# One staging pool for both MLP products, three staging buffers, and another order in the MLP's first block

## The chip, the cores and the metric

The kernel runs on one core of a Trainium2 chip. The metric is the device time of one execution in microseconds. Before the change the median of three runs is 2079.51 us (2078.61 to 2080.41). One further execution was profiled; its rows are what the prediction reads.

The engines that matter are TensorE (PE, with its weight loads shown as PEld), VectorE (DVE), ScalarE (ACT) and SyncE (SP). SP only issues transfers, in the order of its queue: an issue that has to wait for a semaphore holds all that stand behind it.

## The reference, cut to what matters

One layer on 512 tokens with a model width of 2048 and a hidden width of 8192, all float32. Only the convolution mixer is used.

```
h = rms_norm(x, norm_mix)
b, c, v = split(h @ conv_w_in, 3)          # 2048 -> 3 x 2048
m = (b * conv3(c * v)) @ conv_w_out        # 2048 -> 2048
x = x + m
h = rms_norm(x, norm_mlp)
x = x + square(relu(h @ mlp_w1)) @ mlp_w2  # 2048 -> 8192 -> 2048
```

## The kernel before, in words

**Numbers in two halves.** A float32 product is made of three matmuls. Each operand is split into a rounded half "hi" (ACT, line 101) and the remainder "lo" (DVE, line 102), and hi x hi, lo x hi and hi x lo are added up in PSUM. Activations appear in the profile as h, g and f (fhi, flo), weights as r, split into whi and wlo. The split weights live in a ring of three pairs (RING).

**The mixer.** The input projection (lines 284 to 317) and the output projection (lines 330 to 350) use plain products in pieces of 256 output columns. The output projection has eight such blocks. Each adds the residual, scales by the norm's gain, splits the slices of three activation forms, writes the other four forms to DRAM (t_mid, line 348) and adds the squares of the new x to ssq (line 113).

**The MLP's products.** Both MLP products use a Strassen-Winograd scheme of seven quarter products (function `fast`) for a 2 x 2 split of weights and activations. The weights' forms are X11, S1, S2, S4, S3, X12, X22, the activations' forms Y11, T1, T2, Y22, T3, Y21, T4, matched in this order. A quarter product has 8 steps of three matmuls, so 24; a block of 256 output columns has 168. The sums of the weights are made on the fly on DVE (`quarters`, line 173). The first product has 32 blocks (line 368), the second 32 as well: four chunks of the hidden width with eight blocks each.

**Forms of the activations.** Seven forms, each a pair hi and lo of 128 x 2048, have one home each (fa and fb). For the first product Y11, Y21, Y22 are split slice by slice in the output projection, while T1 to T4 are read back from t_mid. For the second product all seven forms of a chunk are read from `hidden`, which the first product's blocks write (line 378): chunk 0 from blocks 0 to 7, and so on. A read (function `read`, line 356) goes into a staging tile f of 1 MB and is split from there into its home. A home can be written once the last matmul with its old contents is done.

**Norm.** The second norm's factor per token (rbc) is not applied to h but to the first product's result (line 372). `token_factors` makes it: one matmul with a matrix of ones adds ssq over the partitions (line 119, the "squares' matmul"), then mean, square root and reciprocal follow with one step of refinement on DVE.

**Buffers.** The first product's block has a result c (two buffers), which is rescaled (line 372), squared into q (line 374), extended by differences (line 217) and written to hidden. Before the change the tiles f and q of the first product share one tag "q" with two buffers in the pool mw. The second product has a pool of its own, vw, opened after mw is closed and lying over the same memory: two buffers for f, two for the residual xt, two for c, and one for the output staging o.

**What sets the order.** The framework plans each engine's order by program order and by when, in its own timing, an instruction's inputs and its buffer are there. So the weight splits of a later block can stand ahead of an earlier block's last steps. On the chip each engine then goes through its list in order, held only by semaphores.

Of the kernel before, what the change touches and what calls it, by code (L numbers as in the profile page):

```python
# [36 lines left out]
def trunk_kernel(  # L37
# [47 lines left out]
    edge.tile([P, 120], F32, name="edge")  # L85
    ident = cst.tile([P, P], F32, name="ident")
    ones = cst.tile([P, P], F32, name="ones")
    rows = cst.tile([5 * KT, P], F32, name="rows")
# [26 lines left out]
    def token_factors(pool):  # L115


        total = bank()
        pe.matmul(total, ones, ssq, start=True, stop=True)
        m = pool.tile([P, S], F32, tag="sq", name="m")  # L120
        t = pool.tile([P, S], F32, tag="sq", name="t")
        dve.tensor_scalar(m, total, 1.0 / D, RMS_EPS, op0=ALU.mult, op1=ALU.add)
        act.activation(t, m, AF.Sqrt)
        dve.reciprocal(rbc, t)
# [3 lines left out]
        dve.tensor_tensor(out=rbc, in0=rbc, in1=t, op=ALU.mult)  # L128
# [58 lines left out]
    def fast(r, forms, c):  # L187
# [5 lines left out]
        for i, (hi, lo) in quarters(r):  # L193
# [31 lines left out]
    cw = es_h.enter_context(tc.tile_pool(name="cw", bufs=2))  # L225

# [19 lines left out]
    with tc.tile_pool(name="xin", bufs=2, side="right", reuse_waits="tile") as xin:  # L246
# [30 lines left out]
        token_factors(cw)  # L277
# [78 lines left out]
    def read(i, src, pool):  # L356

        f = pool.tile([P, NP, HS], F32, tag="q", name="f")
# [5 lines left out]
    with tc.tile_pool(name="mw", bufs=2, reuse_waits="tile") as mw:  # L364
        for i, k in ((T1, 0), (T2, 1), (T3, 2), (T4, 3)):
            forms[i] = read(i, t_mid[:, :, k, :], mw)
        token_factors(mw)
        for n in range(DFF // GC):
            c = mw.tile([P, 2, S], F32, tag="c", name="c")
            fast(load(w1, 0, n * GC), forms, c)  # L370
            r = rbc.unsqueeze(1).to_broadcast([P, 2, S])
            dve.scalar_tensor_tensor(out=c, in0=c, scalar=0.0, in1=r, op0=ALU.max, op1=ALU.mult)
            q = mw.tile([P, 8, HS], F32, tag="q", name="q")
            act.activation(
                q[:, :4, :].rearrange("p q t -> p (q t)"), c.rearrange("p i t -> p (i t)"), AF.Square
            )
            differences(q)
            nc.sync.dma_start(hidden[n // NP][n % NP], q)

    with tc.tile_pool(name="vw", bufs=2, reuse_waits="tile") as vw:  # L380
        def finish(n, c):

            o = vw.tile([P, S // P, GC], F32, tag="o", name="o", bufs=1)
            for b in range(0, S // P, 2):
                pt = bank()
                for i in range(2):
                    for j in range(2):
                        pe.transpose(  # L388
                            pt[:, i * GC + j * P : i * GC + (j + 1) * P],
                            c[:, j, (b + i) * P : (b + i + 1) * P], ident,  # L390
                        )
                act.copy(o[:, b : b + 2, :].rearrange("p b c -> p (b c)"), pt)
            act.dma_start(out[:, n * GC : (n + 1) * GC].rearrange("(b p) c -> p b c", p=P), o)

        done = None
        for ch in range(NCH):
            for i in range(7):
                forms[i] = read(i, hidden[ch][:, :, PLACE[i], :], vw)
            for n in range(NG):
                xt = vw.tile([P, 2, S], F32, tag="xt", name="xt")  # L400
                nc.sync.dma_start(xt.rearrange("p i t -> p (i t)"), x_mid[ch][n])
                c = vw.tile([P, 2, S], F32, tag="c", name="c")
                fast(load(w2, ch * D, n * GC), forms, c)
                dve.tensor_tensor(out=c, in0=c, in1=xt, op=ALU.add)
                if ch < NCH - 1:
                    nc.sync.dma_start(x_mid[ch + 1][n], c.rearrange("p i t -> p (i t)"))
                else:
                    if done:
                        finish(*done)
                    done = n, c  # L410
        finish(*done)


# [28 lines left out]
```

## Time and profile before

| What | us |
|---|---|
| median of three runs | 2079.51 |
| profiled execution | 2078.44 |
| its span, from the first to the last instruction | 2076.7 |
| PE busy | 2025.4 |
| DVE busy | 1418.0 |
| ACT busy | 840.1 |

A row of the timeline has start, length, engine, line, operation, output and inputs, count, and in brackets the idle time before it with what ended it. A row of the waits has the waiting instruction, what it waited for, the total in us, how many times and the longest. A row of the windows has the length of a stretch, and for each engine the busy time and in parentheses the number of instructions; then PE's granted clock as a share of full speed, the DMA engines' busy share and the rate. A row of the groups has the total and after it the mean in ns of one instruction, then the idle time before it.

### The profile page before, as it was taken

The numbers are of one execution on the slowest core, as the hardware profiler recorded it, in microseconds if no ns is written. First come the engines' busy times: TensorE is split into PE (matmuls) and PEld (weight loads), VectorE is DVE, ScalarE is ACT, GpSimd is POOL, SyncE is SP. The second block draws the span as 40 slices with busy tenths as digits, with TensorE's granted clock in tenths as the row PEclk, the third lists the DMA queues.
The fourth block names the chain that finished last, engine by engine and source line by source line (L and its number), as shares of the span: only waits on it lengthen the run. The fifth ranks groups of instructions, "written<-read, shape, count | busy, mean of one in ns | idle before, by whom it ended". The sixth has DMA issues, their size and how long they took to land.

```text
span 2076.7 us, 32835 instructions
## 1 busy us (share of the span) xinstructions
PE 2025.4 (98%) x14001; PEld 1896.6 (91%) x14001; DVE 1418.0 (68%) x1541; ACT 840.1 (40%) x1036; POOL 0.7 (0%) x6
## 2 busy tenths in 40 slices
PE   9999999999999889999999999969999999999998
PEld 7888888888888789999999999968999999999998
DVE  6643333433444588888888887868779779779875
ACT  5322222222333354444444444435445446446443
POOL 0000000000000000000000000000000000000000
PEclk9999999999999999999999999989999999999999
DMA  8323223232354444453434444366448448447441
GB/s 284 122 81 116 87 84 120 81 107 96 131 184 149 163 165 160 148 179 144 163 143 162 164 148 177 143 207 232 148 166 279 168 159 288 163 143 255 141 153 62
DMA packets 260114, 325.13 MB, mean 157 GB/s; under 512 B 9008, under 2 KB 242560, under 8 KB 255872
## 3 DMA queue, kind: packets, MB, share of 16 engines
q1 hardware_dynamic: 255616, 318.80, 44.7%
q10 hardware_dynamic: 4352, 4.24, 0.6%
q8 instruction: 109, 1.79, 0.3%
q14 instruction: 37, 0.30, 0.0%
HBM read 260.09 MB, written 62.91 MB: 156 GB/s over the span
## 4 chain that ended last, share of the span: by engine, by line
PE 92%; DVE 3%; DMA 3%; ACT 1%; issue 1%; SPq 0%; DVEq 0%; ACTq 0%
PE acc L199 20%; PE acc L200 20%; PE acc L198 20%; PE acc L154 11%; PE acc L155 11%; PE acc L153 11%; DMA f<-hidden 1%; DVE flo L102 1%; DVE wlo L102 1%; DMA r<-in_conv_w_in_dram 1%; ACT fhi L101 0%; DVE s L173 0%; DMA r<-in_mlp_w_dram 0%; PE acc L388 0%; ACT whi L101 0%
## 5 line engine op out<-in xcount | busy, mean ns | idle before, releaser
L198 PE MATMUL acc<-fhi,whi 128*128 128x256 f32 x3584 | 1019.2, 285 | 22.4 <-ACT fhi L101 21.1
L199 PE MATMUL acc<-flo,whi 128*128 128x256 f32 x3584 | 1018.0, 284 | 9.5 <-DVE flo L102 9.5
L200 PE MATMUL acc<-fhi,wlo 128*128 128x256 f32 x3584 | 1017.4, 284 | 4.1 <-DVE wlo L102 4.1
L102 DVE TENSOR_TENSOR wlo<-r,whi 128x1024 fp32r<-128x1024 f32 x384 | 468.9, 1223 | 399.2 <-ACT whi L101 389.6
L198 PEld LDWEIGHTS acc<-fhi,whi 128*128 128x128 f32 x3584 | 691.4, 193 | 24.9 <-ACT fhi L101 21.9
L101 ACT CAST whi<-r 128x1024 fp32r<-128x1024 f32 x384 | 403.4, 1051 | 758.2 <-PE acc L154 372.0
L199 PEld LDWEIGHTS acc<-flo,whi 128*128 128x128 f32 x3584 | 691.8, 193 | 11.1 <-DVE flo L102 10.6
L200 PEld LDWEIGHTS acc<-fhi,wlo 128*128 128x128 f32 x3584 | 691.4, 193 | 5.3 <-DVE wlo L102 5.3
L101 ACT CAST whi<-s 128x1024 fp32r<-128x1024 f32 x192 | 201.4, 1049 | 323.0 <-PE acc L199 222.1
L154 PE MATMUL acc<-h_lo,whi 128*128 128x512 f32 x768 | 298.9, 390 | 0.9 <-DVE h_lo L268 0.6
L155 PE MATMUL acc<-h_hi,wlo 128*128 128x512 f32 x768 | 298.8, 389 | 0.3 <-DVE wlo L102 0.3
L153 PE MATMUL acc<-h_hi,whi 128*128 128x512 f32 x768 | 297.8, 390 | 0.6 <-ACT h_hi L267 0.5
L102 DVE TENSOR_TENSOR wlo<-s,whi 128x1024 fp32r<-128x1024 f32 x192 | 234.2, 1222 | 60.9 <-ACT whi L101 60.9
L154 PEld LDWEIGHTS acc<-h_lo,whi 128*128 128x128 f32 x768 | 144.1, 188 | 32.3 <-DVE h_lo L268 2.2
L153 PEld LDWEIGHTS acc<-h_hi,whi 128*128 128x128 f32 x768 | 143.8, 188 | 31.3 <-ACT h_hi L267 1.3
L155 PEld LDWEIGHTS acc<-h_hi,wlo 128*128 128x128 f32 x768 | 144.1, 188 | 30.3 <-DVE wlo L102 0.5
L211 DVE TENSOR_TENSOR c<-acc,c 128x256 f32<-128x256 f32 x192 | 81.4, 424 | 100.3 <-PE acc L200 96.8
L153 PE MATMUL acc<-g_hi,whi 128*128 128x512 f32 x256 | 99.6, 389 | 0.0
L154 PE MATMUL acc<-g_lo,whi 128*128 128x512 f32 x256 | 99.6, 389 | 0.0
L155 PE MATMUL acc<-g_hi,wlo 128*128 128x512 f32 x256 | 99.6, 389 | 0.0
L102 DVE TENSOR_TENSOR flo<-f,fhi 128x2048 fp32r<-128x2048 f32 x32 | 73.2, 2287 | 15.0 <-ACT fhi L101 14.9
L173 DVE TENSOR_TENSOR s<-r 128x1024 f32<-128x1024 f32 x64 | 78.0, 1219 | 4.2 <-DMA r<-in_mlp_w_dram 2.8
(66 smaller groups left out, 1005.1 us busy)
## 6 DMA issues: line engine op xcount, KB each, us to landing
r<-in_mlp_w_dram SPq DMA_DIRECT2D x256, 512.0 KB, 5.5
r<-in_conv_w_in_dram SPq DMA_DIRECT2D x96, 512.0 KB, 5.7
hidden<-q SPq DMA_DIRECT2D x32, 1024.0 KB, 3.8
f<-hidden SPq DMA_DIRECT2D x28, 1024.0 KB, 6.2
r<-in_conv_w_out_dram SPq DMA_DIRECT2D x32, 512.0 KB, 5.3
xt<-x_mid SPq DMA_DIRECT2D x32, 512.0 KB, 4.1
x_mid<-c SPq DMA_DIRECT2D x24, 512.0 KB, 2.9
xn<-in_x_dram SPq DMA_DIRECT2D x16, 256.0 KB, 5.1
```

The costliest lines, as they stand in the source:

```text
L101: act.copy(hi, src)
L102: dve.tensor_tensor(out=lo, in0=src, in1=hi.bitcast(F32), op=ALU.subtract)
L153: pe.matmul(acc[j], hi[:, k, cs], a, start=first, stop=False)
L154: pe.matmul(acc[j], hi[:, k, cs], b, start=False, stop=False)
L155: pe.matmul(acc[j], lo[:, k, cs], a, start=False, stop=last)
L173: dve.tensor_tensor(out=o, in0=a, in1=b, op=op)
L198: pe.matmul(acc, hi[:, k, :], f_hi[:, k, :], start=first, stop=False, skip_group_check=True)
L199: pe.matmul(acc, hi[:, k, :], f_lo[:, k, :], start=False, stop=False, skip_group_check=True)
L200: pe.matmul(acc, lo[:, k, :], f_hi[:, k, :], start=False, stop=last, skip_group_check=True)
L211: dve.tensor_tensor(out=o, in0=acc, in1=o, op=ALU.add)
```

## The change

- The pool mw stays open to the end and serves both products. Its tag "q" now has three buffers and holds f, q and the output staging o. c and xt are tags of the same pool. vw is gone.
- `token_factors` is called after the products of the MLP's first block instead of before them, and takes the tag "xt" for its two temporaries.
- In the MLP's first block only (`early`), X12 with Y21 comes second instead of sixth.
- To make room, `rows` moves into the pool cw, which is closed before the MLP, and a padding tile ("edge") shrinks from 120 to 8 columns.

```diff
-    edge.tile([P, 120], F32, name="edge")
+    edge.tile([P, 8], F32, name="edge")
-    rows = cst.tile([5 * KT, P], F32, name="rows")
...
-    def token_factors(pool):
+    def token_factors(pool, tag):
         total = bank()
         pe.matmul(total, ones, ssq, start=True, stop=True)
-        m = pool.tile([P, S], F32, tag="sq", name="m")
-        t = pool.tile([P, S], F32, tag="sq", name="t")
+        m, t = (pool.tile([P, S], F32, tag=tag, name=n) for n in ("m", "t"))
...
-    def quarters(r):
+    def quarters(r, early):
...
         yield X11, operand(x11, shape)
+        if early:
+            yield X12, operand(x12, shape)
         tt(s_b, s_a, x11)
...
-        yield X12, operand(x12, shape)
+        if not early:
+            yield X12, operand(x12, shape)
         yield X22, operand(x22, shape)
...
     cw = es_h.enter_context(tc.tile_pool(name="cw", bufs=2))
+    rows = cw.tile([5 * KT, P], F32, name="rows", bufs=1)
...
-        f = pool.tile([P, NP, HS], F32, tag="q", name="f")
+        f = pool.tile([P, NP, HS], F32, tag="q", name="f", bufs=3)
...
-    with tc.tile_pool(name="mw", bufs=2, reuse_waits="tile") as mw:
-        for i, k in ((T1, 0), (T2, 1), (T3, 2), (T4, 3)):
-            forms[i] = read(i, t_mid[:, :, k, :], mw)
-        token_factors(mw)
-        for n in range(DFF // GC):
+    mw = ctx.enter_context(tc.tile_pool(name="mw", bufs=2, reuse_waits="tile"))
+    for i, k in ((T1, 0), (T2, 1), (T3, 2), (T4, 3)):
+        forms[i] = read(i, t_mid[:, :, k, :], mw)
+    for n in range(DFF // GC):
+        c = mw.tile([P, 2, S], F32, tag="c", name="c")
+        fast(load(w1, 0, n * GC), forms, c, early=n == 0)
+        if n == 0:
+            token_factors(mw, "xt")
...
+        q = mw.tile([P, 8, HS], F32, tag="q", name="q", bufs=3)
...
-    with tc.tile_pool(name="vw", bufs=2, reuse_waits="tile") as vw:
...
-            o = vw.tile([P, S // P, GC], F32, tag="o", name="o", bufs=1)
+        o = mw.tile([P, S // P, GC], F32, tag="q", name="o", bufs=3)
...
-                forms[i] = read(i, hidden[ch][:, :, PLACE[i], :], vw)
+            forms[i] = read(i, hidden[ch][:, :, PLACE[i], :], mw)
-                xt = vw.tile([P, 2, S], F32, tag="xt", name="xt")
+            xt = mw.tile([P, 2, S], F32, tag="xt", name="xt")
-                c = vw.tile([P, 2, S], F32, tag="c", name="c")
+            c = mw.tile([P, 2, S], F32, tag="c", name="c")
```

More of the change, by code (lines that the diff above doesn't have):

```diff
@@ L183, in quarters, with fast @@
         yield S3, operand(x21, shape)
-        yield X12, operand(x12, shape)
+        if not early:
+            yield X12, operand(x12, shape)
         yield X22, operand(x22, shape)
-    def fast(r, forms, c):
+    def fast(r, forms, c, early=False):
         bx, by, bz = (bank()[:, :HS] for _ in range(3))
@@ L192, in fast @@
         t0, t1 = slice(0, HS), slice(HS, S)
-        for i, (hi, lo) in quarters(r):
+        for i, (hi, lo) in quarters(r, early):
             acc = sums[i]
@@ L276, in trunk_kernel @@
                 unit(acc_n[i], r_n[i], c * XK, h_hi, h_lo, k_first=c == 0)
-        token_factors(cw)
+        token_factors(cw, "sq")
     with tc.tile_pool(name="gp", bufs=1, side="right", reuse_waits="tile") as gp:
@@ L362, in read @@
         return made
-    with tc.tile_pool(name="mw", bufs=2, reuse_waits="tile") as mw:
-        for i, k in ((T1, 0), (T2, 1), (T3, 2), (T4, 3)):
-            forms[i] = read(i, t_mid[:, :, k, :], mw)
-        token_factors(mw)
-        for n in range(DFF // GC):
-            c = mw.tile([P, 2, S], F32, tag="c", name="c")
[L370 to L378, printed above, removed]
@@ L380, in trunk_kernel @@
-    with tc.tile_pool(name="vw", bufs=2, reuse_waits="tile") as vw:
-        def finish(n, c):
-            o = vw.tile([P, S // P, GC], F32, tag="o", name="o", bufs=1)
[L384 to L397, printed above, removed]
-                forms[i] = read(i, hidden[ch][:, :, PLACE[i], :], vw)
-            for n in range(NG):
-                xt = vw.tile([P, 2, S], F32, tag="xt", name="xt")
-                nc.sync.dma_start(xt.rearrange("p i t -> p (i t)"), x_mid[ch][n])
-                c = vw.tile([P, 2, S], F32, tag="c", name="c")
[L403 to L411, printed above, removed]
@@ new lines, in trunk_kernel @@
+    mw = ctx.enter_context(tc.tile_pool(name="mw", bufs=2, reuse_waits="tile"))
[6 more added lines that the diff above has]
+            token_factors(mw, "xt")
+        r = rbc.unsqueeze(1).to_broadcast([P, 2, S])
+        dve.scalar_tensor_tensor(out=c, in0=c, scalar=0.0, in1=r, op0=ALU.max, op1=ALU.mult)
+        q = mw.tile([P, 8, HS], F32, tag="q", name="q", bufs=3)
+        act.activation(
+            q[:, :4, :].rearrange("p q t -> p (q t)"), c.rearrange("p i t -> p (i t)"), AF.Square
+        )
+        differences(q)
+        nc.sync.dma_start(hidden[n // NP][n % NP], q)
@@ new lines, in finish @@
+    def finish(n, c):
+        o = mw.tile([P, S // P, GC], F32, tag="q", name="o", bufs=3)
+        for b in range(0, S // P, 2):
+            pt = bank()
+            for i in range(2):
+                for j in range(2):
+                    pe.transpose(
+                        pt[:, i * GC + j * P : i * GC + (j + 1) * P],
+                        c[:, j, (b + i) * P : (b + i + 1) * P], ident,
+                    )
+            act.copy(o[:, b : b + 2, :].rearrange("p b c -> p (b c)"), pt)
+        act.dma_start(out[:, n * GC : (n + 1) * GC].rearrange("(b p) c -> p b c", p=P), o)
@@ new lines, in trunk_kernel @@
+    done = None
+    for ch in range(NCH):
+        for i in range(7):
+            forms[i] = read(i, hidden[ch][:, :, PLACE[i], :], mw)
+        for n in range(NG):
+            xt = mw.tile([P, 2, S], F32, tag="xt", name="xt")
+            nc.sync.dma_start(xt.rearrange("p i t -> p (i t)"), x_mid[ch][n])
+            c = mw.tile([P, 2, S], F32, tag="c", name="c")
+            fast(load(w2, ch * D, n * GC), forms, c)
+            dve.tensor_tensor(out=c, in0=c, in1=xt, op=ALU.add)
+            if ch < NCH - 1:
+                nc.sync.dma_start(x_mid[ch + 1][n], c.rearrange("p i t -> p (i t)"))
+            else:
+                if done:
+                    finish(*done)
+                done = n, c
@@ L415 @@
+    finish(*done)
 _INS = [
```

## The prediction

> **What bounds the kernel now.** I read the busy times first, then the waits of the matmul engine, then windows over the places where it waits.
>
> ```profile
> PE 2025.4 (98%) x14001; PEld 1896.6 (91%) x14001; DVE 1418.0 (68%) x1541; ACT 840.1 (40%) x1036; POOL 0.7 (0%) x6
> ...
> PE acc L198 <- ACT fhi L101: 21.1, 4, 16.9
> PE acc L119 <- DVE ssq L113: 5.0, 1, 5.0
> ```
>
> PE is the bound nearly everywhere, so only its holes can be won. The largest are waits for a split operand (fhi); one is the squares' matmul waiting for its sum. Windows size each hole (columns: start and end, length, then busy time and count of PE, PEld, DVE, ACT, POOL, granted clock, DMA share, GB/s):
>
> ```profile
> 770.00:1370.00 600.00, 600.00 (x5002) 600.00 (x5002) 497.84 (x568) 279.51 (x359) 0.00 (x0) 1.00 0.44 157
> ...
> 715.60:752.30 36.70, 25.60 (x171) 24.12 (x171) 32.00 (x33) 18.06 (x20) 0.00 (x0) 0.86 0.46 158
> 1357.10:1427.20 70.10, 46.54 (x338) 45.24 (x337) 47.60 (x45) 31.53 (x31) 0.00 (x0) 0.81 0.64 215
> 1548.30:1611.90 63.60, 61.28 (x504) 60.47 (x504) 59.98 (x53) 37.74 (x40) 0.00 (x0) 1.00 0.80 264
> 1709.80:1773.50 63.70, 62.55 (x517) 61.90 (x516) 60.53 (x53) 38.88 (x41) 0.00 (x0) 1.00 0.82 272
> 1871.00:1938.00 67.00, 64.15 (x525) 62.98 (x524) 61.54 (x54) 38.31 (x41) 0.00 (x0) 1.00 0.67 222
> ```
>
> Undisturbed, a matmul takes 600/5002 = 0.12 us, a block of 168 takes 20.16, a quarter product of 24 takes 2.88. Length minus count times 0.12 is what each stretch loses: entry of the MLP (first MLP block) 16.2 us, first product to second 29.5, and the three later changes of hidden chunk 3.1, 1.7 and 4.0. Each of these five places is touched by the change.
>
> **Part 1: the first MLP block.** The kernel before puts the squares' matmul (L119) ahead of X11.
>
> ```profile
> 716.78 0.41 DVE L102 TENSOR_TENSOR flo<-q,fhi 128x256 fp32r<-128x256 f32 x1
> 718.58 0.75 DVE L102 TENSOR_TENSOR flo<-q,fhi 128x256 fp32r<-128x256 f32 x2
> 720.66 1.81 PE L119 MATMUL acc<-ssq,ones 128*128 128x512 f32 x2 [4.95 <-DVE ssq L113]
> 729.91 0.39 PE L198 MATMUL acc<-fhi,whi 128*128 128x256 f32 x1 [3.67 <-ACT fhi L101]
> 732.76 0.58 PE L199 MATMUL acc<-flo,whi 128*128 128x256 f32 x1 [2.47 <-DVE flo L102]
> ...
> 720.03 0.34 SPq L348 DMA_DIRECT2D t_mid<-q  x1
> 722.79 13.11 SPq L359 DMA_DIRECT2D f<-t_mid  x4
> ...
> 727.95 1.90 ACT L101 CAST fhi<-f 128x2048 fp32r<-128x2048 f32 x1 [0.48 <-DMA f<-t_mid]
> 730.62 1.90 ACT L101 CAST fhi<-f 128x2048 fp32r<-128x2048 f32 x1 [0.77 <-DMA f<-t_mid]
> ...
> 724.35 3.35 DVE L124 RECIPROCAL rbc<-t 128x512 f32<-128x512 f32 x1 [0.74 <-ACT t L123]
> 730.42 2.29 DVE L102 TENSOR_TENSOR flo<-f,fhi 128x2048 fp32r<-128x2048 f32 x1
> ...
> L128 DVE TENSOR_TENSOR rbc<-rbc,t 128x512 f32<-128x512 f32 x2 | 1.4, 692 | 0.1
> L102 DVE TENSOR_TENSOR wlo<-r,whi 128x1024 fp32r<-128x1024 f32 x384 | 468.9, 1223 | 399.2 <-ACT whi L101 389.6 <-PE acc L264 6.6 <-PE acc L119 2.4
> ```
>
> The output projection ends at 720.66 - 4.95 = 715.7. X11 needs Y11, whose last slice is there at 717.2, and X11 reaches that slice only after 21 matmuls, at 718.2. So X11 and X12 (Y21's last slice at 719.3) run 715.7 to 721.5. The chain that ends the hole does not move: last differences written at 720.03, T1 requested at 722.79, cast to 729.85, low part from 730.42 (0.5 us sooner if VectorE is free) to 732.7. PE then stands 721.5 to 732.5, and S1 starts as before. X12's 24 matmuls no longer stand behind S1: -2.9, and up to -0.5 from the low part. The squares' matmul costs PE nothing if it falls into the gap between S1's first and second matmul, where its bank is next; 0.9 (half of 1.81) if it comes last.
>
> X12's operands move ahead of S1's in the ring of three: X11, X12, S1 are split while the projection still runs, S2 and S4 take the places of X11 and X12 at 718.6 and 721.5, inside the hole. If that cover were gone, a split of 1.05 + 1.22 would show.
>
> The norm's chain on VectorE is the reciprocal (3.35) and five operations of at most 0.69: up to 6.8. It began while PE stood. Now it needs the squares' matmul, which comes after S1's first, so it runs inside the block, and the weight splits and the rescale of the first c are queued behind it. From 730 to 752 VectorE has four low parts (9.2), the chain (6.8), five weight splits (6.1) and about 2.5 of sums and additions (estimated as two more such splits): 24.6 in 22. So 0 to 2.6 come back; I take 1. If the whole chain were exposed, 6.8 would. Part 1: **-2.4**, between -3.9 and +3.9. T3 no longer waits for a buffer, but PE has no hole at T3 now, so that is worth nothing; the work that hides it is S1 and S2.
>
> **Part 2: first product to second.** Now f of hidden chunk 0 lies in a pool that opens over the first product's buffers.
>
> ```profile
> 1365.44 0.34 SPq L378 DMA_DIRECT2D hidden<-q  x1
> 1371.05 2.63 SPq L136 DMA_DIRECT2D r<-in_mlp_w_dram  x4
> 1384.54 0.34 SPq L378 DMA_DIRECT2D hidden<-q  x1
> 1384.98 5.04 SPq L359 DMA_DIRECT2D f<-hidden  x2
> ...
> 1396.66 20.84 SPq L359 DMA_DIRECT2D f<-hidden  x5
> ...
> 1380.82 1.06 ACT L374 ACTIVATE q<-c 128x1024 f32<-128x1024 f32 x1 [2.16 <-DVE c L372]
> ...
> 1384.06 0.42 DVE L217 TENSOR_TENSOR q<-q 128x256 f32<-128x256 f32 x1
> ...
> 1396.69 0.58 PE L199 MATMUL acc<-flo,whi 128*128 128x256 f32 x1 [1.75 <-DVE flo L102]
> 1406.99 0.57 PE L199 MATMUL acc<-flo,whi 128*128 128x256 f32 x1 [2.26 <-DVE flo L102]
> ...
> 1407.00:1410.40 3.40, 3.40 (x16) 3.40 (x17) 3.28 (x2) 0.31 (x1) 0.00 (x0) 0.51 0.61 189
> ...
> hidden<-q SPq DMA_DIRECT2D x32, 1024.0 KB, 3.8
> f<-hidden SPq DMA_DIRECT2D x28, 1024.0 KB, 6.2
> ```
>
> The first read of chunk 0, whose data were written 23 blocks earlier, stands on SP behind the last write of hidden (1384.54), and the other five each wait for one of two buffers. With one pool, the order in which the planner hands out buffers of a tag decides. L119 above is the clue: it stands ahead of X11 although X11's operands were complete 3.5 us sooner, so banks are given in order of first use. By that order the first two reads follow the last block's Square (ACT 1380.82) in the plan and go ahead of the last write on SP. SP itself has nothing to wait for there: the previous writes are long landed (1365.44 + 3.8), so they issue when the weight loads are through, at 1373.7.
>
> Two reads of T1 and T2 landed 2.7 us apart (727.95, 730.62), so I estimate 2.7 us per MB. Two MB of weights from 1371.05 and two of f land at about 1380 and 1383. ACT does Square until 1381.9, then the casts until 1383.8 and 1385.7; VectorE is free at 1384.5, the low parts are done at 1386.8 and 1389.1. X11 runs from 1386.8 instead of 1396.69: 9.9 us.
>
> After that, three buffers. X11 at half clock (16 matmuls in 3.4 us by the window row instead of 1.9) ends at 1391.2, S1 at 1394.1. The third read takes the first buffer at 1386.8, lands 6.2 later, and is split 4.2 later, at 1397.2: a hole of 3.1, another 1.5 of half clock, S2 ends at 1401.5. The fourth and fifth were issued at 1388.4 (1384.54 + 3.8) and 1389.1 and are there in time. The sixth and seventh take buffers at 1397.2 and 1399.9 and are ready at 1407.6 and 1410.3; X22 ends at 1413.4. VectorE's work of the stretch (47.60 in 70.10) is squeezed into 58, so I add 2: 1415.4 against 1427.3. Part 2: **-12**, between -6 (reads stay behind the write, third buffer alone) and -26 (the change costs only what a later change of chunk costs).
>
> The Trainium skill, "TensorE: Matmul & The Clock Gate", section "Why this matters for your kernels", lets the clock fall only for gaps over about 3 us. Here a gap of 2.26 us was followed by 3.4 us at clock 0.51, so the measurement decides against it. By the rule the hole of 3.1 us before S2 stands at the edge, and the sum would be up to 1.5 lower.
>
> **Part 3: the three later changes of chunk.**
>
> ```profile
> 1560.00:1600.00 40.00, 37.68 (x308) 36.87 (x307) 38.45 (x34) 24.45 (x25) 0.00 (x0) 1.00 0.98 326
> ...
> ACT fhi L101 <- DMA f<-hidden: 4.4, 2, 2.8
> ...
> ACT fhi L101 <- DMA f<-hidden: 7.1, 4, 2.4
> ```
>
> The reads are already early here. A third buffer removes the casts' waits for them (4.4 and 7.1 us at the first and third change), but VectorE is busy 38.45 of 40 us and DMA 0.98, so little of it reaches PE. Of 8.8 us lost in all I take **-2**, between -6 and +3 (one more read in flight in front of the weights, 1 us each).
>
> **Part 4: the end.** The output staging o has one buffer before and three now.
>
> ```profile
> 2068.82 0.38 ACTq L393 DMA_DIRECT2D out_dram<-o  x1
> 2068.97 1.09 PE L388 MATMUL acc<-ident,c 128*128 128x128 f32 x8 [0.85 <-DVE c L404]
> 2071.68 1.07 ACT L392 COPY o<-acc 128x512 f32<-128x512 f32 x2 [2.88 <-DMA out_dram<-o]
> ```
>
> The last copies wait for the previous output to leave. Without it they start when the first four transposes are through, near 2069.7: **-1.9**, between -2.2 and -1. The moves of rows and of the padding tiles change no instruction: zero, since they are addresses only.
>
> **Sum.** -2.4 - 12 - 2 - 1.9 = -18.3. The profiled execution took 2078.44 (span 2076.7 and 1.7 around it), so it becomes 2060.1; the median of the runs lies 1.07 above the profiled one, so the forecast is 2061.2.
>
> **Rivals.**
> - *Reads far ahead.* If a read takes any free buffer, chunk 0 is staged long before and this change costs 3 us like the others: -26 in part 2, 2047. Against it: three reads taken at block 8 would hold all three buffers until the last block frees the forms, and block 8's q would never get one.
> - *It doesn't do what it says:* the first read is still planned behind the last write (for it: it stands there today, 0.44 us behind). Then only the third buffer counts: -6 in part 2, 2067. Against it: today two pools force that order.
> - *No gain in either MLP place,* the norm's chain exposed (+3.9), part 2 at -6, the later changes at +3, the end -1.9: -1.0, 2078.5. VectorE's load speaks for it; that each price is the far end of its bound speaks against it.
> - *Slower: weight loads stuck behind reads on SP.* A read that waits for its buffer holds the in-order queue (the five reads of the fence hold it 20.84 us). The weights of block 33 are issued at 1371.05; block 33 could start two blocks after 1357.1, at 1397.4, and they need 6 to land and 5 for sums and splits, so about 16 us of lateness is free. It decides from there: held 26 us at each of the last three changes, PE waits 10 each, +30 - 18.3, 2091. Against it: the queue has stood that long already, and a third buffer shortens each wait.
>
> **How the numbers follow.** Forecast 0.70 (own range 2052 to 2069); reads far ahead 0.08; first read still behind 0.12; no gain 0.05; slower 0.05. A measurement of this kernel tells about 0.2% (4 us) from no change, so faster is below 2075.3: 0.70 + 0.08 + 0.12 = 0.90; same 0.05; slower 0.05. The range of 8 in 10 leaves out the far-ahead case and the two bad ones: 2050 to 2070.
>
> **What would show it.** Part 1: X11 directly behind the projection without a wait, L119 in or after S1, one wait of about 11 us before S1, block 1 near 750. Part 2: two reads of hidden on SP ahead of the last write, X11's wait about 9 us instead of 17, then holes under 3 us. Part 3: VectorE still near full at the changes. Part 4: the last copies not waiting for the output. The prediction is wrong if the first read is issued long before block 31, or if reads stand ahead of weights and PE waits for whi.

## The result, and the profile after

| | before | after |
|---|---|---|
| median (lowest to highest), us | 2079.06 (2076.66 to 2080.41) | 2043.93 (2039.87 to 2045.94) |
| profiled execution, us | 2078.44 | 2044.67 |
| its span, us | 2076.7 | 2042.9 |

With one further run, the median before the change is of four. The ratio is 0.983, with a 95% interval of 0.9812 to 0.9848: 35 us faster, where 18 were forecast (2061.2, range 2050 to 2070). The direction was right, the time lies outside the range. The line numbers after the change: the three matmuls of a quarter product are L200 to L202 (L198 to L200 before), the split is L100 and L101 (L101 and L102 before).

Windows show where the 35 us come from. In the kernel before, the first row is a stretch in which PE has no hole, the second the output projection, then the two blocks in which each hidden chunk changes (columns as in the prediction: length, busy time and count of PE, PEld, DVE, ACT, POOL, granted clock, DMA share, GB/s):

```profile
775.00:1330.00 555.00, 555.00 (x4628) 555.00 (x4627) 460.75 (x526) 258.76 (x332) 0.00 (x0) 1.00 0.44 156
541.50:715.50 174.00, 174.00 (x769) 143.93 (x767) 80.28 (x116) 59.02 (x85) 0.00 (x0) 1.00 0.47 163
1568.41:1612.08 43.67, 41.35 (x339) 40.54 (x337) 40.44 (x37) 22.35 (x26) 0.00 (x0) 1.00 0.84 280
1733.04:1775.36 42.32, 41.16 (x338) 40.52 (x337) 40.34 (x37) 22.54 (x26) 0.00 (x0) 1.00 0.87 288
1896.32:1941.76 45.44, 42.59 (x347) 41.42 (x345) 41.28 (x37) 23.10 (x27) 0.00 (x0) 1.00 0.66 216
```

The same view of the kernel after; the third row is its first MLP block, the fourth the two blocks around the change from the first product to the second:

```profile
775.00:1330.00 555.00, 555.00 (x4780) 555.00 (x4778) 473.11 (x543) 267.99 (x343) 0.00 (x0) 1.00 0.45 161
541.60:720.50 178.90, 178.90 (x768) 143.41 (x767) 79.95 (x116) 59.20 (x85) 0.00 (x0) 1.00 0.46 159
720.79:755.75 34.96, 24.81 (x171) 22.41 (x170) 31.52 (x33) 18.01 (x19) 0.00 (x0) 0.85 0.56 195
1341.31:1400.08 58.77, 44.76 (x339) 43.47 (x337) 48.39 (x45) 31.48 (x31) 0.00 (x0) 0.88 0.73 251
1536.77:1584.13 47.36, 42.17 (x339) 41.57 (x338) 41.55 (x38) 21.20 (x25) 0.00 (x0) 0.93 0.75 260
1701.24:1748.62 47.38, 41.77 (x338) 41.17 (x337) 41.51 (x38) 21.51 (x25) 0.00 (x0) 0.93 0.75 259
1865.74:1913.70 47.96, 42.45 (x346) 41.64 (x345) 42.32 (x38) 21.98 (x26) 0.00 (x0) 0.96 0.54 187
```

The first rows hold the surprise. PE is busy without a hole in both, at a granted clock of 1.00, and yet the kernel after does 4780 matmuls in the 555 us and the kernel before 4628: 116.1 ns each instead of 119.9. The matmul itself became faster in the MLP. In the output projection it became slower, 178.90/768 = 232.9 ns against 174.00/769 = 226.3.

The timeline of PE in the kernel after shows that it isn't every matmul (start, length, engine, line). Each row is the first of a step's three; the first two rows belong to X12, with Y21, and stand one step apart, the last two to X22, with T4:

```profile
1357.01 0.28 PE L200 MATMUL acc<-fhi,whi 128*128 128x256 f32 x1
...
1357.37 0.28 PE L200 MATMUL acc<-fhi,whi 128*128 128x256 f32 x1
...
1358.79 0.28 PE L200 MATMUL acc<-fhi,whi 128*128 128x256 f32 x1
...
1359.13 0.28 PE L200 MATMUL acc<-fhi,whi 128*128 128x256 f32 x1
```

Three matmuls with Y21 take 0.36 us, as all did before; three with T4 take 0.34. All three quarters that read Y forms (X11, S4, X12) keep 120 ns, the four that read T forms (S1, S2, S3, X22) run at 113.3. A block is 3 x 24 x 0.1197 + 4 x 24 x 0.1133 = 19.5 us instead of 20.16. T forms and g lie on the right side of the memory, Y forms, h and the split weights on the left. The change moved the sides against each other, as the sizes in the diff tell: `rows`, 128 columns of 4 bytes, left the left side, so all behind it moves by -512 bytes; `edge` lost 112 columns of 4, so all on the right moves by +448. In the kernel before all of them lie a multiple of 512 bytes from the split weights, in a partition. The change takes this offset of T forms and g from 0 to -64 bytes modulo 512. That of Y forms and h stays 0.

With 168 matmuls a block, the length of a window less its blocks at the undisturbed pace (20.16 or 19.52 each) is what a place loses. That gives the account between the two profiled executions:

| place | before, lost | after, lost | difference |
|---|---|---|---|
| 64 blocks at the undisturbed pace | 64 x 20.16 | 64 x 19.52 | -41.0 |
| output projection | 768 x 0.2263 | 768 x 0.2329 | +5.1 |
| first MLP block | 16.6 | 15.4 | -1.1 |
| first product to second | 29.9 | 19.7 | -10.1 |
| three later changes of chunk | 3.4 + 2.0 + 5.1 | 8.3 + 8.3 + 8.9 | +15.1 |
| end, after the last matmul of a block | 9.7 | 7.7 | -2.0 |

The sum is -34.0, the profiled executions differ by 33.8. (Each difference is taken before rounding.)

The change from the first product to the second is nearly as forecast. SP's queue and the timeline of PE of the kernel after:

```profile
1354.92 2.21 SPq L134 DMA_DIRECT2D r<-in_mlp_w_dram  x4
1357.18 4.31 SPq L362 DMA_DIRECT2D f<-hidden  x2
1368.47 0.33 SPq L382 DMA_DIRECT2D hidden<-q  x1
```

```profile
720.54 0.39 PE L153 MATMUL acc<-g_hi,wlo 128*128 128x512 f32 x1
720.77 0.28 PE L200 MATMUL acc<-fhi,whi 128*128 128x256 f32 x1
...
734.56 0.58 PE L200 MATMUL acc<-fhi,whi 128*128 128x256 f32 x1 [7.88 <-ACT fhi L100]
734.94 1.91 PE L118 MATMUL acc<-ssq,ones 128*128 128x512 f32 x2
...
1369.28 0.58 PE L200 MATMUL acc<-fhi,whi 128*128 128x256 f32 x1 [8.29 <-ACT fhi L100]
...
1541.96 0.58 PE L202 MATMUL acc<-fhi,wlo 128*128 128x256 f32 x1 [4.56 <-DVE wlo L101]
```

Two reads stand ahead of the last write, right behind the weight loads. X11 stands directly behind the projection, and the squares' matmul falls behind S1's first. At the end the last copies wait 0.87 us for PE and no longer for the output to leave:

```profile
2037.92 1.07 ACT L395 COPY o<-acc 128x512 f32<-128x512 f32 x2 [0.87 <-PE acc L391]
```

The last row of PE's timeline above is the new loss at a later change of chunk: PE waits 4.56 us for the low part of a weight. VectorE in the kernel after, there:

```profile
1535.15 4.48 DVE L101 TENSOR_TENSOR flo<-f,fhi 128x2048 fp32r<-128x2048 f32 x2
1539.56 1.22 DVE L407 TENSOR_TENSOR c<-c,xt 128x1024 f32<-128x1024 f32 x1
1540.69 1.22 DVE L101 TENSOR_TENSOR wlo<-r,whi 128x1024 fp32r<-128x1024 f32 x1
```

In the kernel before, at the same change, one low part of f stands there, and PE's longest hole is 1.17 us:

```profile
1568.50 2.29 DVE L102 TENSOR_TENSOR flo<-f,fhi 128x2048 fp32r<-128x2048 f32 x1
1570.71 1.22 DVE L404 TENSOR_TENSOR c<-c,xt 128x1024 f32<-128x1024 f32 x1
1571.85 2.35 DVE L102 TENSOR_TENSOR wlo<-s,whi 128x1024 fp32r<-128x1024 f32 x2
```

```profile
1580.06 0.38 PE L200 MATMUL acc<-fhi,wlo 128*128 128x256 f32 x1 [1.17 <-DVE wlo L102]
```

### The profile page after: what moved, and what is told of

Same layout as the page of the kernel before. It is cut to its first block, busy times and chain, and to the rows that moved or that the text cites. A ratio compares the mean times of both kernels' runs of the same rounds, so it can differ in the third digit from the quotient of the medians.

```text
span 2042.9 us, 32807 instructions
## 1 busy us (share of the span) xinstructions
PE 1994.1 (98%) x14001; PEld 1859.8 (91%) x14001; DVE 1417.5 (69%) x1541; ACT 841.7 (41%) x1036; POOL 0.7 (0%) x6
## 4 chain that ended last, share of the span: by engine, by line
PE 91%; DVE 3%; DMA 3%; ACT 1%; issue 1%; SPq 0%; DVEq 0%; ACTq 0%
PE acc L200 19%; PE acc L202 19%; PE acc L201 19%; PE acc L152 11%; PE acc L153 11%; PE acc L151 11%; DVE flo L101 1%; DMA f<-hidden 1%; DVE wlo L101 1%; DMA r<-in_mlp_w_dram 1%; DMA r<-in_conv_w_in_dram 1%; ACT whi L100 1%; ACT fhi L100 0%; PE acc L391 0%; DMA f<-t_mid 0%
## 5 line engine op out<-in xcount | busy, mean ns | idle before, releaser
L200 PE MATMUL acc<-fhi,whi 128*128 128x256 f32 x3584 | 1007.0, 281 | 18.8 <-ACT fhi L100 16.5
L202 PE MATMUL acc<-fhi,wlo 128*128 128x256 f32 x3584 | 1005.4, 281 | 16.2 <-DVE wlo L101 16.2
L201 PE MATMUL acc<-flo,whi 128*128 128x256 f32 x3584 | 1004.5, 280 | 5.4 <-DVE flo L101 5.4
L101 DVE TENSOR_TENSOR wlo<-r,whi 128x1024 fp32r<-128x1024 f32 x384 | 469.2, 1223 | 395.3 <-ACT whi L100 386.2
L100 ACT CAST whi<-r 128x1024 fp32r<-128x1024 f32 x384 | 404.9, 1055 | 738.0 <-PE acc L152 381.3
L200 PEld LDWEIGHTS acc<-fhi,whi 128*128 128x128 f32 x3584 | 683.5, 191 | 20.5 <-ACT fhi L100 17.1
L202 PEld LDWEIGHTS acc<-fhi,wlo 128*128 128x128 f32 x3584 | 682.7, 191 | 17.9 <-DVE wlo L101 17.9
L201 PEld LDWEIGHTS acc<-flo,whi 128*128 128x128 f32 x3584 | 683.0, 191 | 7.9 <-DVE flo L101 7.9
L100 ACT CAST whi<-s 128x1024 fp32r<-128x1024 f32 x192 | 202.4, 1054 | 319.7 <-PE acc L201 228.7
L101 DVE TENSOR_TENSOR wlo<-s,whi 128x1024 fp32r<-128x1024 f32 x192 | 234.9, 1224 | 51.9 <-ACT whi L100 51.9
L172 DVE TENSOR_TENSOR s<-r,s 128x1024 f32<-128x1024 f32 x64 | 78.4, 1225 | 2.0
```

Of the source, the lines that this page charges most:

```text
L100: act.copy(hi, src)
L101: dve.tensor_tensor(out=lo, in0=src, in1=hi.bitcast(F32), op=ALU.subtract)
L200: pe.matmul(acc, hi[:, k, :], f_hi[:, k, :], start=first, stop=False, skip_group_check=True)
L201: pe.matmul(acc, hi[:, k, :], f_lo[:, k, :], start=False, stop=False, skip_group_check=True)
L202: pe.matmul(acc, lo[:, k, :], f_hi[:, k, :], start=False, stop=last, skip_group_check=True)
```

## The experiments

The letters of the theories are those of each expectation. Below, "offset" is the distance of an activation operand from the split weights in a partition, in bytes modulo 512. A pace is the distance of matmul starts in an undisturbed stretch of the timeline. The kernel before, run beside them, had medians of 2079.03, 2080.71, 2080.95 and 2081.02 us on the four occasions.

### The addresses alone

The kernel before with the small edge tile, and nothing else:

```diff
-    edge.tile([P, 120], F32, name="edge")
+    edge.tile([P, 8], F32, name="edge")
```

> The kernel before with one edit: the padding tile edge has 8 columns in place of 120, so that everything on the right side of the memory (T1 to T4's forms, g, the first inputs) lies 448 bytes higher and nothing else changes. Theory A (place): the pace of a matmul depends on where its moving operand starts; 64 bytes below a multiple of 512 a matmul of 256 columns takes 113.3 ns in place of 120, and one of 512 columns 233 in place of 227. Then the quarters S1, S2, S3, X22 take 2.72 to 2.74 us, a block 19.52, the output projection is about 5 us longer, and the whole is 2079 - 41 + 5 and some 0 to 15 given back at the changes of chunk: 2043 to 2058. Theory B (work): the gain comes from the shared pool, the third buffer and the new order. Then nothing changes here: 2079, block 20.16.

Measured: 2047.32 us (2046.24 to 2052.91), ratio 0.9853 (0.9833 to 0.9874). Its windows, the stretch without holes, the first product to the second, and the first later change of chunk:

```profile
775.00:1330.00 555.00, 555.00 (x4780) 555.00 (x4779) 473.17 (x543) 267.64 (x343) 0.00 (x0) 1.00 0.45 161
1341.49:1411.83 70.34, 46.56 (x339) 45.27 (x337) 47.74 (x45) 31.65 (x31) 0.00 (x0) 0.81 0.65 217
1548.33:1591.83 43.50, 40.75 (x338) 39.57 (x337) 40.73 (x37) 22.57 (x26) 0.00 (x0) 1.00 0.85 282
```

One line that moves addresses, with every instruction as before, gives 31.7 of the 35 us, as theory A has it. The pace is the 4780 matmuls of the kernel after, and the first product to the second loses 70.34 - 39.04 = 31.3, a little more than the 29.9 of the kernel before. Of the 41 us of pace, 5 go to the output projection and some 4 to the changes of product and of chunk, where PE waits for other engines, so that a faster PE waits longer.

### The change without its addresses

The kernel after with the old edge tile:

```diff
-    edge.tile([P, 8], F32, name="edge")
+    edge.tile([P, 120], F32, name="edge")
```

> The changed kernel with the padding tile edge back at 120 columns: all of the shared pool, three buffers and the new order, without the move of the right side. Theory A (place): block 20.16 us, output projection at 227 ns a matmul, and the time that the prediction's own terms give, 2061 (2055 to 2067). Theory B (work): as the changed kernel, 2044.

Measured: 2074.69 us (2072.67 to 2077.91), ratio 0.9977 (0.9967 to 0.9986). Its windows, the stretch without holes, the first MLP block, the first product to the second, the three later changes:

```profile
775.00:1330.00 555.00, 555.00 (x4627) 555.00 (x4626) 459.56 (x525) 257.93 (x332) 0.00 (x0) 1.00 0.44 156
714.78:750.08 35.30, 25.80 (x171) 23.41 (x170) 31.63 (x33) 17.94 (x19) 0.00 (x0) 0.81 0.56 197
1354.88:1413.39 58.51, 44.70 (x339) 43.40 (x337) 48.35 (x46) 31.67 (x31) 0.00 (x0) 0.88 0.74 251
1554.51:1602.04 47.53, 42.78 (x338) 41.97 (x337) 41.07 (x37) 20.71 (x25) 0.00 (x0) 0.96 0.75 256
1723.00:1770.54 47.54, 43.25 (x338) 42.84 (x337) 41.07 (x37) 20.70 (x25) 0.00 (x0) 0.93 0.73 255
1891.50:1939.83 48.33, 43.62 (x346) 42.72 (x345) 41.84 (x37) 21.41 (x26) 0.00 (x0) 0.96 0.53 181
```

The pace is the old one, as theory A has it; its 2055 to 2067 us did not come, because it took the prediction's own terms as right. This kernel is the test of the prediction's own terms, since here they stand alone: first block -1.4, first product to second 58.51 - 40.32 = 18.2 instead of 29.9, so -11.7, later changes 7.2 + 7.2 + 8.0 = 22.4 instead of 10.5, so +12, end -2.0. What the early reads win, the later changes lose. 4.3 us are left.

### Weights and left side moved by 64 bytes

```diff
-    cst.tile([P, 224], F32, name="lead")
+    cst.tile([P, 208], F32, name="lead")
```

in the kernel before. Weights, Y forms and h move together; T forms and g stay where they are, and come to lie at +64 from the weights.

> The kernel before with the padding tile lead at 208 columns in place of 224: everything on the left side (weights, h, Y11, Y22, Y21) lies 64 bytes lower, the right side stays. Theory A1 (the moving operand's own place counts): X11, S4, X12 go to 2.72 us (-0.48 us a block, -31 over 64 blocks), S1, S2, S3, X22 stay at 2.88, the input projection goes to 233 ns a matmul (2304 x 6 ns, +14), the changes of chunk give back 0 to 10: 2062 to 2072. Theory A2 (the place relative to the weights counts): X11, S4, X12 and the input projection stay as they are, and S1, S2, S3, X22 and the output projection may change. Theory B (work): nothing changes, 2079.

Measured: 2072.07 us (2070.7 to 2077.34), ratio 0.997 (0.996 to 0.9981). The stretch without holes:

```profile
775.00:1330.00 555.00, 555.00 (x4672) 555.00 (x4671) 464.52 (x530) 261.34 (x335) 0.00 (x0) 1.00 0.46 157
```

The Y quarters keep 119.9 ns although they moved, the T quarters go to 117.8 although they didn't; of the projections, h keeps 227 and g goes from 226.7 to 228.9. Theory A2 held. What counts is the place relative to the tiles on the left, with the weights the ones that a matmul reads. An absolute place of the activations is excluded.

### Part 1 undone

The kernel after with the squares' matmul ahead of the first block and X12 back in sixth place:

```diff
+    token_factors(mw, "xt")
     for n in range(DFF // GC):
...
-        fast(load(w1, 0, n * GC), forms, c, early=n == 0)
-        if n == 0:
-            token_factors(mw, "xt")
+        fast(load(w1, 0, n * GC), forms, c)
```

> The changed kernel with its first edit undone: the squares' matmul ahead of the first block's products again and X12 in sixth place. Theory: this edit is worth little, since the read of T1 ends the hole in both; the entry of the MLP (from the end of the output projection to the second block, without one undisturbed block of 19.52) goes from 15.5 back to 16.6 us, between 16 and 18.5. Rival (the prediction's own working: X12's 24 matmuls leave the path): 18 or more. Elsewhere as the changed kernel: the whole 2045 to 2048.

Measured: 2044.84 us once. The first block's window:

```profile
720.64:756.65 36.01, 25.60 (x172) 23.93 (x171) 32.09 (x33) 17.92 (x20) 0.00 (x0) 0.81 0.61 214
```

It is 1.05 us longer than the 34.96 of the kernel after. The block loses 36.01 - 19.52 = 16.5 us, so the theory held and the rival (18 or more) did not: part 1 is worth about 1 us there. In the total it can't be told from a single run.

### Two buffers instead of three

The kernel after with `bufs=2` for f, q and o of the tag "q":

```diff
-        f = pool.tile([P, NP, HS], F32, tag="q", name="f", bufs=3)
+        f = pool.tile([P, NP, HS], F32, tag="q", name="f", bufs=2)
```

> The changed kernel with two buffers of the staging tag in place of three (f, q and o). Theory C (the third buffer does harm at the later changes of chunk, because a second read's low part is then ready early and goes ahead of the low part of the weights on VectorE): the losses of the three changes fall from 8.3, 8.3 and 8.9 us to between 3 and 5 each, and first product to second loses more than 19.7, some 22 to 27 us, since one read fewer is staged ahead: the whole 2035 to 2043. Rival D (the one pool does it, not the third buffer): the later changes stay at 8 and the whole rises to 2047 to 2053.

Measured: 2043.6 us once. The first MLP block, the first product to the second, the first later change:

```profile
720.75:753.36 32.61, 23.66 (x171) 21.48 (x170) 30.10 (x31) 17.89 (x19) 0.00 (x0) 0.84 0.51 173
1338.95:1407.90 68.95, 48.52 (x339) 46.54 (x337) 49.14 (x46) 31.58 (x31) 0.00 (x0) 0.83 0.67 225
1544.50:1589.09 44.59, 41.06 (x338) 39.56 (x337) 40.83 (x37) 22.73 (x26) 0.00 (x0) 1.00 0.83 274
```

The third buffer is worth 10.2 us between the products (68.95 against 58.77) and costs 2.3 in the first block (34.96 against 32.61) and 2.8, 3.0 and 3.1 at the later changes. The sum is +1.0, and the total is that of three buffers: taken together, the third buffer wins nothing here. Rival D is refuted, since the later changes did not stay at 8. Theory C had the direction and not the sizes: the three changes lose 5.6, 5.3 and 5.9 (3 to 5 expected), and between the products 68.95 - 39.04 = 29.9 us are lost (22 to 27 expected). On SP one read of chunk 0 still stands ahead of the last write of hidden, and yet the 29.9 are only 1.4 less than the 31.3 of the kernel before with the new addresses. So the third buffer made most of part 2, and the early read by itself little. A third buffer without the early reads was not run. Against that same kernel, which loses 4.5, 4.2 and 4.9 at the later changes, two buffers lose 3 us more in all and three buffers 12, so the third buffer also made most of the loss of part 3.

### All forms at the better offset

The kernel after with a pad of 112 columns ahead of the Y forms and one ahead of g. All seven forms lie at -64, g at 0 again:

```diff
+        gp.tile([P, 112], F32, name="gpad")
...
+        fa.tile([P, 112], F32, name="fpad")
```

> The changed kernel with two more padding tiles of 112 columns: one ahead of Y11, Y22, Y21 in their pool, which puts them 64 bytes below a multiple of 512 as T1 to T4 are, and one behind g, which puts g back on a multiple of 512. Theory A (place): all seven quarters take 2.72 us, a block 19.05 (-0.45 on 64 blocks, -29), the output projection 227 ns a matmul (-5), the changes of chunk give back 0 to 9: 2010 to 2019. Theory B (work): 2044.

Measured: 2020.71 us (2015.56 to 2025.52), ratio 0.9728 (0.9705 to 0.975). The stretch without holes:

```profile
775.00:1330.00 555.00, 555.00 (x4899) 555.00 (x4899) 484.33 (x556) 273.88 (x351) 0.00 (x0) 1.00 0.47 166
```

113.3 ns in every quarter of this stretch, and the output projection is back at 226.7. The time is just above the 2010 to 2019 of theory A, and theory B is refuted. Two pads without work give 23 us more here; a second run of the same kernel, at the end of this section, gives 11. In the last chunk five of its eight blocks (58 and 60 to 63, counted from 0 over both products) ran at 117.8.

### Reads held back in the program order

The kernel with the two pads, with each form's read called right ahead of its own quarter in a chunk's first block (inside `fast`) instead of all seven ahead of the block:

```diff
+            if fetch:
+                forms[i] = fetch(i)
...
-        for i in range(7):
-            forms[i] = read(i, hidden[ch][:, :, PLACE[i], :], mw)
+        def fetch(i):
+            return read(i, hidden[ch][:, :, PLACE[i], :], mw)
...
-            fast(load(w2, ch * D, n * GC), forms, c)
+            fast(load(w2, ch * D, n * GC), forms, c, fetch=None if n else fetch)
```

> The changed kernel with the two padding tiles of the earlier run (Y11, Y22, Y21 64 bytes below a multiple of 512, g on one), and with each form's read of a new chunk called in the chunk's first block right ahead of the quarter product that needs it, and not all seven ahead of the block; the same reads into the same three buffers. Theory C (order on VectorE): the low part of the weights now stands ahead of a later form's low part, the changes of chunk fall from 9 us to 3 to 5 each and first product to second from 19.8 to 16 to 20: 2000 to 2010, against 2020.7 for the pads alone. Rival E (VectorE has too much to do in any order there): no change from 2020.7, between 2017 and 2025.

Measured: 2014.43 us (2002.72 to 2035.19), ratio 0.9646 (0.961 to 0.9682), the lowest median of all. It lies between what theory C (2000 to 2010) and rival E (2017 to 2025) expected. The first later change, in this kernel's window and then in that of the kernel without the edit:

```profile
1525.18:1568.30 43.12, 40.44 (x339) 39.15 (x337) 41.20 (x37) 22.23 (x25) 0.00 (x0) 1.00 0.90 306
```

```profile
1512.80:1559.69 46.89, 41.64 (x338) 41.24 (x337) 41.78 (x38) 21.64 (x25) 0.00 (x0) 0.93 0.78 262
```

With blocks of 19.04 us, the three later changes lose 5.0, 6.6 and 4.8 us instead of 8.8, 9.1 and 9.2. Nothing but the order of the reads and splits differs, so that order costs 10.7 of these 27.1 us. Between the products nothing was won: the two blocks took 58.84 us, and 57.90 without the edit. The total is less sure than the windows, since the pace changed within this execution: blocks 1 to 15 ran at 113.3 ns a matmul, 17 to 31 at 117.8, 33 to 58 at 113.3 outside the changes, and 59 to 63 at 117.8. Two stretches of it without holes, blocks 5 to 14 and 18 to 29:

```profile
827.10:1017.50 190.40, 190.40 (x1683) 190.40 (x1682) 166.06 (x191) 93.95 (x120) 0.00 (x0) 1.00 0.47 166
1075.70:1313.10 237.40, 237.40 (x2019) 237.40 (x2017) 199.16 (x229) 112.69 (x144) 0.00 (x0) 1.00 0.45 160
```

The first slowing came in the middle of block 16, within the quarter S3 and without a hole: the starts there are 113 or 114 ns apart, then once 132, then 117 to 119.

### Other offsets

Three kernels are the kernel after with other pads, each run once; the sizes below are of edge, the pad ahead of h, of g and of the Y forms, in columns:

```
 offsets Y +128, T -128, h +128, g -160:  edge 24, hpad 32, gpad 8, fpad 32
 offsets Y +256, T -192, h +256, g -288:  edge 40, hpad 64, gpad 24, fpad 64
 offsets Y +32, T -32, h +32, g -32:      no edge tile, hpad 8, fpad 8
```

> The changed kernel with its operands moved by padding tiles, for the pace of matmuls alone. Offsets of the moving operand from the weights, modulo 512 bytes: Y11, Y22, Y21 at +128, T1 to T4 at -128, h at +128, g at -160. So far 256 columns took 120.0 ns at 0, 117.8 at +64 and 113.3 at -64; 512 columns took 226.7 at 0, 228.9 at +64 and 233.3 at -64. Theory F (the offset matters in steps of 64 with a period under 512): both quarters' paces are among 113.3, 117.8 and 120.0. Theory G (only one 64 byte window is special): 120.0 in both and 226.7 in both.

Measured: 2082.8 us. 118.6 ns in all quarters, 232.4 for h and 233.3 for g. Neither theory has that: 118.6 is none of the three paces of theory F, and not the 120.0 of theory G.

> The kernel after with other places: the Y forms lie 256 bytes above a multiple of 512 away from the weights, the T forms 192 below one, h 256 above and g 288 below; the work is the same. Theory A (the pace depends on the distance from a multiple of 512 alone, is best near 64 bytes and goes back to the old 120 ns as the distance grows, as 64: 113.3 or 117.8, 128: 118.6 have it): 119 to 120 ns a matmul in all quarters, block 20.0 to 20.16 us, 2072 to 2085 us. Theory B (only the side counts: operands below the multiple are fast, above it slow): T quarters (4 of 7) below 117.8 ns, Y quarters above 118, block near 19.6, 2045 to 2055 us.

Measured: 2068.08 us. Y quarters 119.9, T quarters 117.8, h 226.7, g 233.3. Neither theory fits: +256 acts like 0, and -192 like the +64 of the moved weights. Both follow if places count modulo 256.

> The kernel after with the Y forms and h 32 bytes above a multiple of 512 away from the weights, the T forms and g 32 below one. Theory A (distance alone, best near 64 and old pace at 0): between the two, 113.3 to 118.6 ns in all quarters alike, block 19.0 to 19.9 us, 2015 to 2070 us. Theory B (only the side counts): T quarters at 113.3 to 117.8 ns, Y quarters at 118 to 120, two paces within a block, block 19.4 to 19.9. Theory C (places count in steps of 64 bytes): as at 0, 120 ns, block 20.16, near 2075 us.

Measured: 2077.0 us. Y quarters 116.7, T quarters 118.4, h and g 233.3. No theory fits: the two paces differ, and the side above is the faster one. The blocks are faster (19.78 us); the input projection, 2304 matmuls with h at 6.6 ns more each, takes 15 us of that back.

### Period of 256 bytes

All forms at +192, which is -64 modulo 256, h and g at 0; the kernel after with

```diff
-    edge.tile([P, 8], F32, name="edge")
+    edge.tile([P, 72], F32, name="edge")
...
+        gp.tile([P, 48], F32, name="gpad")
...
+        fa.tile([P, 48], F32, name="fpad")
```

> The kernel after with all seven forms 192 bytes above a multiple of 512 away from the weights, h and g on a multiple; the work is the same. Theory D (places count modulo 256 bytes: 256 above behaved like 0 with 119.9 ns, 192 below like 64 above with 117.8, so 192 above is 64 below): 113.3 ns in all quarters, block 19.04 us, 2015 to 2026 us, and 117.8 ns where the pace switches as it did in the run with the later reads, at most 2060. Theory A (distance from a multiple of 512, pace back towards 120 from 128 bytes on): 118 to 120 ns, block 19.9 to 20.1, 2068 to 2080 us.

Measured: 2017.26 us (2016.14 to 2039.89), ratio 0.9732 (0.9672 to 0.9791). The stretch without holes:

```profile
775.00:1330.00 555.00, 555.00 (x4900) 555.00 (x4899) 483.63 (x556) 273.95 (x351) 0.00 (x0) 1.00 0.47 166
```

Theory D held: 113.3 ns in all quarters of this stretch. That the pace goes back to 120 with the distance from a multiple of 512 is refuted. (Blocks 58 and 60 to 63 ran at 117.8 here too.)

> The same kernel as the one with all seven forms 64 bytes below and g on a multiple of 512, once more, beside the one with 192 above. Pace fixed by the place: 113.3 ns in all quarters and 2015 to 2026 us again. Pace that switches at this place: some blocks near 117.8 ns, a median up to 2060, or a spread of more than 10 us between executions.

This is the kernel with all forms at -64 ("All forms at the better offset") once more. Measured, beside the one at +192: 2032.96 us (2019.73 to 2044.88), ratio 0.977 (0.9708 to 0.9833). The profiled execution took 2021.62. Its windows of five blocks each in hidden chunk 0 and in chunk 1:

```profile
1400.30:1499.20 98.90, 98.90 (x842) 98.90 (x841) 77.17 (x76) 42.18 (x55) 0.00 (x0) 1.00 0.48 160
1565.30:1660.50 95.20, 95.20 (x842) 95.20 (x841) 77.26 (x76) 42.27 (x55) 0.00 (x0) 1.00 0.49 166
```

The same 842 matmuls, without a hole, at clock 1.00, at the same addresses: 117.5 ns and 113.1. Chunk 0 fell to the slower pace within its first block and kept it until the next change of chunk. A pace fixed by the place is refuted for this offset: it has two, and PE kept each of them for many blocks. The executions near 2044 us were not profiled, so that they spent more blocks at the slower pace is likely and not shown.

## Why the prediction was right and wrong

**The step that failed** is the last sentence of part 4: "The moves of rows and of the padding tiles change no instruction: zero, since they are addresses only." The premise holds, the conclusion doesn't. Undone alone in the kernel after, the move of the right side is worth 31 us (2074.69 against 2043.93), done alone in the kernel before 32 (2047.32 against 2079.03). Nothing in the profile of before showed that price, since all operands lay at offset 0 there. But every other term of the sum has a bound on both sides, and this one got a zero without a bound.

**A second step failed, hidden by the first:** part 3, -2 between -6 and +3. Measured +12 at the old pace, +15 at the new one. The rows quoted for it held the reason, VectorE 38.45 of 40 us: with three buffers, two casts of f are through at once, VectorE makes both low parts back to back (4.48 us), and the low part of a weight, 1.22 us of work that PE needs, stands behind them. The +3 priced a read ahead of the weights in the DMA queue; the thing to price was a low part of f ahead of a weight's on VectorE: 2.3 us, and after it PE at half clock. The slow clock shows in the same windows: 0.93 to 0.96 after, 1.00 before. The loss of the three changes falls from 25.6 to 16.7 us with two buffers, and from 27.1 to 16.4 with the reads held back. The kernel before with the new addresses lost 13.5, so a rest of about 3 us is not explained.

**Part 1**, -2.4: measured -1.1 to -1.4. X11 and X12 run directly behind the projection, the squares' matmul comes behind S1's first, and there is one wait of 7.88 us ahead of S1; with the 0.4 us of S1's first matmul and the 1.9 of L118 it makes the "about 11". With the old addresses block 1 starts at 750.1, for "near 750". The -2.4 contains +1 for the norm's chain, but what came back is something else. In the kernel after, VectorE makes two low parts of f back to back behind the chain's reciprocal, and the low parts of two weights stand behind them:

```profile
742.96 4.42 DVE L101 TENSOR_TENSOR flo<-f,fhi 128x2048 fp32r<-128x2048 f32 x2
747.63 2.35 DVE L101 TENSOR_TENSOR wlo<-r,whi 128x1024 fp32r<-128x1024 f32 x2
```

PE waits 0.82 us for the high part of a weight and 1.37 for a low part, and from 748.46 to 751.88 it runs at half clock. The kernel with two buffers has the same reciprocal, but a weight's low part comes first behind it:

```profile
742.86 1.16 DVE L101 TENSOR_TENSOR wlo<-r,whi 128x1024 fp32r<-128x1024 f32 x1
743.94 2.28 DVE L101 TENSOR_TENSOR flo<-f,fhi 128x2048 fp32r<-128x2048 f32 x1
```

There the block loses 32.61 - 19.52 = 13.1 us, 3.5 less than before the change and 2.9 less than the kernel before with the new addresses (16.0). Without the norm's chain -2.9 to -3.4 were forecast, so the chain itself gave back 0.5 at most. The step that failed here is "T3 no longer waits for a buffer [...] so that is worth nothing": the third buffer costs 2.3 us in this block, in the same way as in part 3. (The lower bound of -3.9 is not in the working; its terms give -2.9 - 0.5 = -3.4.)

**Part 2**, -12: measured -11.7 at the old pace, -10.1 in the kernel after. The clue of L119, that places are handed out in order of first use, gave the right order on SP: two reads behind the weights, ahead of the last write. X11's wait of "about 9" is 8.29. The hole before S2, put at 3.1, is one of 0.35 and one of 2.26 around S2's first matmul. But the prediction gave the order 6 of the 12, and in the kernel with two buffers, where one read stands ahead of the write, it won 1.4; order and third buffer work together. The rival with reads far ahead, and the one in which the first read stays behind the write, are refuted by SP's rows.

**Part 4**, -1.9: measured -2.0, by the mechanism that was forecast.

With the addresses undone the sum of the terms comes to -3.1, where -18.3 was forecast: parts 1, 2 and 4 off by 1 or less, part 3 by 14. So the forecast would have been wrong without the addresses as well, by 13.5 us to the other side (2074.69 against 2061.2); two misses of opposite signs make it look nearer than its working was. The rival "no gain in either MLP place" came near that time for other reasons: part 2 did gain.

The gap of 2.26 us that the prediction read against the Trainium skill ("TensorE: Matmul & The Clock Gate", section "Why this matters for your kernels", which speaks of gaps over about 3 us) came up again after the change, before S2's second matmul in hidden chunk 0, with 0.35 us of waiting before S2's first; the 4.4 us behind it:

```profile
1382.50:1386.90 4.40, 4.37 (x24) 4.37 (x25) 4.40 (x3) 2.15 (x2) 0.00 (x0) 0.61 0.74 222
```

The granted clock there is 0.61, so the trace differs from the rule again. In the first MLP block even the two waits of 0.82 and 1.37 us, 0.5 us apart, were enough to see it fall: it is 0.50 from 748.46 to 751.88.

## What to carry to other kernels

"Only addresses move" is no reason for a zero: when a change adds, drops or resizes any tile, work out how the operands of the hot matmuls move against each other, and time an unchanged kernel with that shift alone. Where an engine behind the bound one is nearly full at a change of stage, a deeper buffer lets it do more of one kind of work in a row, and what the bound engine needs next waits behind that; price the row of work, not the buffer. Here the third buffer won 10 us at one place and lost 11 at four others. When a result has the right sign, undo its parts one by one before believing the terms: here two misses half cancelled.

## What the runs showed of the hardware

The distance of matmul starts depends on the offset between the activation operand and the split weights. All rows are of undisturbed stretches at a granted clock of 1.00, in ns a matmul; the offset is modulo 256, which holds for every pair that was run (for 256 columns 0 and +256, +64 and -192, -64 and +192; for 512 columns 0 and +256). The rows of 512 columns are the input and output projections, those of 256 the MLP's products:

| offset mod 256 | 256 columns | 512 columns |
|---|---|---|
| 0 | 120.0 | 226.7 |
| 32 | 116.7 | 233.3 |
| 64 | 117.8 | 228.9 |
| 96 | not run | 233.3 |
| 128 | 118.6 | 232.4 |
| 192 | 113.3, at times 117.8 | 233.3 |
| 224 | 118.4 | 233.3 |

For 256 columns offset 0 is the slowest place that was run and for 512 columns the fastest, so one layout for both gains in one stage and pays in the other. The best kernels here put h and g at 0 and all forms at -64. At that place the pace isn't settled: 113.3 or 117.8 ns, mostly taken up at a change of stage, once in the middle of an undisturbed block, and kept for many blocks; in all four profiled kernels with all forms there, blocks 60 to 63 ran at 117.8. Single executions of one kernel spread over 25 us (2019.73 to 2044.88), where the kernel before, on the same occasion, stays within 7 (2077.41 to 2084.23). What in the memory or in PE makes the offset count, and what decides between the two paces, stays open: the runs show that they depend on these, not why.
